# Before the layer norms of a two-layer trunk: three weight tiles kept, the second half's last products in two narrow banks, epsilon added early

## The chip, the core and the metric

The kernel runs on one core of a Trainium2 chip. The engines that matter are TensorE (PE in the profile; its weight loads are listed apart as PEld), VectorE (DVE), ScalarE (ACT), GpSimd (POOL) and SyncE (SP), whose queue issues nearly all transfers from memory. The metric is device time in microseconds, the median of several runs. Products add up in PSUM, which this kernel uses as eight banks of 512 columns (f32); everything else lies in SBUF.

## The reference, cut to what matters

One sequence of 256 tokens with 2048 features goes through two layers. Each layer has a token mixer (forgetting attention in layer 0, sliding-window attention in layer 1) and a gated feed-forward block with a short convolution. Behind each of these four sublayers stands a residual with a gate and a layer norm:

```python
x = layer_norm(DEEPNORM_ALPHA * x + (1.0 + g1) * y, ln_mix_g[i], ln_mix_b[i])
h = x * (1.0 + sc2) + sh2
y = conv_ffn(h, ...)
x = layer_norm(DEEPNORM_ALPHA * x + (1.0 + g2) * y, ln_ffn_g[i], ln_ffn_b[i])

def layer_norm(x, g, b):
    mu = jnp.mean(xf, axis=-1, keepdims=True)
    var = jnp.mean(jnp.square(xf - mu), axis=-1, keepdims=True)
    y = (xf - mu) * lax.rsqrt(var + LN_EPS)
    return y * g + b
```

`y` is the output of a matrix product (`w_o` of the mixer, `w_down` of the feed-forward block) with 2048 columns. The next sublayer's products need the normalised, modulated `h`, transposed. So at each of the four places all work of the next sublayer hangs on the last columns of the sublayer before. The fourth norm is followed by the output.

## The kernel before

**Tiles.** The tokens are two halves of 128 rows, `t = 0` and `t = 1` (`NT = 2`). Weights come in tiles of 256 x 512 (`wtile`, pool `wp` with ten slots, line 50). A tile holds two blocks of 128 rows and is called a pair here. Every f32 weight is split into a rounded high part and a remainder: ACT casts the tile to `wh` (line 285), VectorE subtracts to get `wl` (line 296), and both have four slots each in the pool `hl` (line 51). A product is then the sum of three: high by high, low by high, high by low (`x_mm`, lines 310 to 331). For one pair and one `t` that is six matmuls of 512 columns.

**The stream.** `stream` (line 277) issues a pair's transfer and its cast and puts its products into the list `work`; `settle` takes them from there with two pairs' lead, and emits the subtraction (`residual_`) some places ahead. Each `go` also makes one step of the list `post` (deferred work, such as the residual behind a product) and of `ada_tick`. The latter works on the modulation vectors in the background: one transfer `wa` and one VectorE accumulation into `acc` per step (lines 434 to 441). The next sublayer's transfers and casts are thus emitted before the last products of the present one. `spare` in `stream` puts `h` and `l` of the last `spare` pairs into the weight pool `wp` instead of `hl`.

**Order.** The tile framework schedules by priority, which is program order, with a model of the time, and sets all waits itself. `pin` keeps an instruction in program order among the pinned ones; others may be moved past them.

**The end of a product.** For the last of the four column blocks before a norm, `x_mm_end` (line 333) holds back the last `n` pairs: `t = 0` gets all its products first, then `t = 1` gets its products of the `n` pairs that were kept. `n` is 2 in `out_proj` (line 786) and in the first layer's feed-forward block, 6 in the second layer's (line 1162), where `spare` is 2.

**Residual and norm.** `residual` (line 654) does for each `t` of a column block of 512: a multiplication of the PSUM bank by the gate (line 660), an addition to `x` (661) and `bn_stats` (663), which gives count, mean and sum of squared deviations for the even and the odd elements. In the last block follow `bn_aggr` to mean and variance (666), the addition of epsilon (668), for `t = 0` the negated mean (670), the power -1/2 on POOL (671), and for `t = 0` on ACT the product of both (673). Only `t = 0` uses that product: it is normalised on ACT (`normalise`, line 687), `t = 1` on VectorE (line 689).

**The start of the next sublayer.** `modulate` (line 534) has a fixed, pinned order on PE: ten filler matmuls on ones (`warm`, tile name `warm`), the four transposes of `t = 0` (line 545), six fillers, the four transposes of `t = 1`, two fillers, then the first products. ACT (512) and VectorE (513, 516) turn the transposes into `hH` and `hL`. The rest of the features follow pair by pair between the products (`feed_`). Behind it, `affine` (line 700) loads rows of the norm's weights (`ln`, line 696) into four slots of `wp`.

**The output.** Behind the fourth norm, lines 1186 to 1195 do two VectorE operations per `t` and block of 512 (1190, 1194) and store the result; nothing there is pinned.

**PSUM.** `x_banks` takes two banks, one for each `t`, for a column block.

Of the kernel before, what the change touches and what calls it, by code (L numbers as in the profile page):

```python
# [10 lines left out]
F32 = mybir.dt.float32  # L11
# [3 lines left out]
ALU = mybir.AluOpType  # L15
AX = mybir.AxisListType

P = 128
D = 2048
# [13 lines left out]
EPS = 1e-5  # L33
# [8 lines left out]
def hybrid_trunk(ctx: ExitStack, tc: tile.TileContext, a: dict, out: bass.AP):  # L42
# [20 lines left out]
    def ttile(name="t"):  # L63
        return tp.tile([P, 2 * S], F32, tag="t", name=name)
# [7 lines left out]
    def x_banks():  # L72
        return [bank("xs") for _ in range(NT)]

    def mm(o, lhsT, rhs, start=False, stop=False, **kw):
        return nc.tensor.matmul(o, lhsT, rhs, start=start, stop=stop, **kw)  # L76
# [233 lines left out]
    def x_mm(ps, kc, h, l, stat, last, first=0, ts=range(NT)):  # L310

        if fresh[0]:
            fresh[0] = False
            for w in (h, l):
                for i in range(2):
                    for t in ts:
                        mm(ps[t], stat(kc + i, t)[0], w[:, i, :], start=w is h and kc + i == first)
            feed()
            for i in range(2):
                for t in ts:  # L320
                    mm(ps[t], stat(kc + i, t)[1], h[:, i, :], stop=kc + i == last)
            return
        for t in ts:
            for i in range(2):
                xh, xl = stat(kc + i, t)
                mm(ps[t], xh, h[:, i, :], start=kc + i == first)
                mm(ps[t], xl, h[:, i, :])
        feed()
        for t in ts:
            for i in range(2):  # L330
                mm(ps[t], stat(kc + i, t)[0], l[:, i, :], stop=kc + i == last)

    def x_mm_end(ps, stat, nk, n):

        kept = []

        def use(kc, h, l):
            end = kc >= nk - 2 * n
            x_mm(ps, kc, h, l, stat, nk - 1, ts=(0,) if end else range(NT))
            if end:  # L340
                kept.append((kc, h, l))
            if kc + 2 >= nk:
                for e in kept:
                    x_mm(ps, *e, stat, nk - 1, ts=(1,))

        return use

    def w_mm(ps, kc, h, l, last=KC - 1, first=0):
# [6 lines left out]
        for i, f, o in cells:  # L355
            mm(o, l[:, i, f * P:(f + 1) * P], hH[:, kc + i, :], stop=kc + i == last, skip_group_check=True)

    def x_stationary(wsrc, col, k0, nk, stat, end=0):

        ps = x_banks()  # L360
        use = x_mm_end(ps, stat, nk, end) if end else lambda kc, h, l: x_mm(ps, kc, h, l, stat, nk - 1)
        stream(wsrc, k0, col, list(range(nk)), use, max(end - 4, 0))
        return ps

    def w_stationary(wsrc, col):
# [279 lines left out]
                due = lambda cb=cb, acc=acc: chunk(cb, acc, bank("cps"))  # L645


    stats = cst.tile([P, NT, D // 512, nc.vector.BN_STATS_DIM], F32, name="stats")
    mhalf = cst.tile([P, 1], F32, name="mhalf")
    nc.gpsimd.memset(mhalf, -0.5)  # L650

# [2 lines left out]
    def residual(ps, d, gate, last):  # L654
        c0 = d * 512
        end = last and d == D // 512 - 1
        for t in range(NT):
            tmp = ttile()
            xs = x[:, t, c0:c0 + 512]
            pin(nc.vector.tensor_tensor(tmp, ps[t], gate[:, c0:c0 + 512], op=ALU.mult), end)  # L660
            pin(nc.vector.tensor_tensor(xs, xs, tmp, op=ALU.add), end)
            if last:
                pin(nc.vector.bn_stats(stats[:, t, d, :], xs), end)
            if end:
                mv = sp.tile([P, 2], F32, tag="mv", name="mv")
                pin(nc.vector.bn_aggr(mv, stats[:, t].rearrange("p a b -> p (a b)")))
                rs = sp.tile([P, 2], F32, tag="rs", name="rs")
                pin(nc.vector.tensor_scalar_add(rs[:, 0:1], mv[:, 1:2], EPS))
                if t == 0:
                    pin(nc.vector.tensor_scalar_mul(rs[:, 1:2], mv[:, 0:1], -1.0))  # L670
                nc.gpsimd.tensor_tensor(rs[:, 0:1], rs[:, 0:1], mhalf, op=ALU.pow)
                if t == 0:
                    nc.scalar.mul(rs[:, 1:2], rs[:, 1:2], rs[:, 0:1])
                moments[t] = (mv[:, 0:1], rs[:, 0:1], rs[:, 1:2])
            yield
# [101 lines left out]
    def out_proj(oT, full, w_o, l):  # L777
        def stat(kc, t):
            while kc not in full:
                step()  # L780
            return oT[kc][0][:, t * P:(t + 1) * P], oT[kc][1][:, t * P:(t + 1) * P]

        ps = {d: x_banks() for d in range(2)}

        def part(d, ks):
            use = x_mm_end(ps[d], stat, KC, 2) if d == D // WB - 1 else                 lambda kc, h, l_: x_mm(ps[d], kc, h, l_, stat, KC - 1)
            stream(w_o, 0, d * WB, ks, use)

        for i, ks in enumerate((range(0, 8), range(8, 12))):
            then(lambda i=i: ada.update(rate=((1.4,1.4,1.8,1.8), (0.9,)*4)[l][i]))  # L790
            for d in range(2):
                part(d, list(ks))
        then(lambda: ada_need(l, 2))
        for d in range(D // WB):
            if d < 2:
                part(d, list(range(12, KC)))
            else:
                then(lambda d=d: ada.update(rate=((1.4,1.4,1.8,1.8), (0.9,)*4)[l][d]))
                ps[d] = x_banks()
                part(d, list(range(KC)))  # L800
            then(lambda d=d: defer(residual(ps[d], d, gates[l, 2], True)))
        then(lambda: (flush(), ada.update(gate_free=True)))
# [293 lines left out]
    def conv_ffn(l):  # L1096
# [42 lines left out]
        for si, (b0, b1) in enumerate(sbs):  # L1139
            gT = []  # L1140
            then(lambda: ada.update(rate=(0.52, 0.4)[l]))
            for b in range(b0, b1):
                ps = w_stationary(w_up, b * WB)
                sil = [ttile("sil") for _ in range(2)]
                then(lambda ps=ps, b=b, sil=sil: defer(evac(ps, b * 4, silu(sil))))
                ps = w_stationary(w_up, DFF + b * WB)
                then(lambda ps=ps, b=b, sil=sil, gT=gT: defer(evac(ps, DFF // P + b * 4, gated(sil, gT))))

            def stat(kc, t, gT=gT):
                while kc >= len(gT):  # L1150
                    run_post()
                return gT[kc][:, 0, t * P:(t + 1) * P], gT[kc][:, 1, t * P:(t + 1) * P]

            def ready(si=si):
                if si == 0:
                    drain()
                ada_need(l, 5)
                ada["rate"] = (0.8, 0.4)[l]

            then(ready)  # L1160
            for d in range(D // WB):
                ps = x_stationary(w_dn, d * WB, b0 * 4, (b1 - b0) * 4, stat, (2, 6)[l] if si > 0 and d == D // WB - 1 else 0)
                then(lambda ps=ps, d=d, si=si: defer(residual(ps, d, gates[l, 5], si == len(sbs) - 1)))
        then(lambda: (flush(), ada.update(gate_free=True)))

# [56 lines left out]
```

## Time and profile before

| | us |
|---|---|
| median of 3 runs | 2248.07 (2247.27 to 2249.3) |
| the profiled execution | 2247.84 |
| its span, first to last instruction | 2246.1 |

The profile page shows one execution; its span is 1.74 us shorter than the time of that execution, which covers what lies around the instructions. Busy times overlap between engines. A group's line in the profile gives line, engine, operation, output and input, sizes, count, then busy time, mean duration in ns, the idle time of the engine just before, and what ended it. In the timeline the columns are start, duration, engine, line, operation, tiles, sizes, count, and in brackets the idle time before with its releaser; instructions of one kind are merged, and a merged entry's duration runs from the first start to the last end. The chain that ended last is followed back from the last instruction, each step to what released it, or to the instruction before it on its engine.

### The profile page before, as it was taken

The numbers are of one execution on the slowest core, as the hardware profiler recorded it, in microseconds if no ns is written. First come the engines' busy times: TensorE is split into PE (matmuls) and PEld (weight loads), VectorE is DVE, ScalarE is ACT, GpSimd is POOL, SyncE is SP. The second block draws the span as 40 slices with busy tenths as digits, with TensorE's granted clock in tenths as the row PEclk, the third lists the DMA queues.
The fourth block names the chain that finished last, engine by engine and source line by source line (L and its number), as shares of the span: only waits on it lengthen the run. The fifth ranks groups of instructions, "written<-read, shape, count | busy, mean of one in ns | idle before, by whom it ended". The sixth has DMA issues, their size and how long they took to land.

```text
span 2246.1 us, 33371 instructions
## 1 busy us (share of the span) xinstructions
PE 2199.2 (98%) x12206; PEld 1890.7 (84%) x12206; DVE 1854.0 (83%) x2689; ACT 1194.2 (53%) x1873; POOL 19.9 (1%) x51
## 2 busy tenths in 40 slices
PE   6999999999999999999999999999999999999997
PEld 6988998788888888888888788888888888888886
DVE  7989998889988968978988989889988655676766
ACT  4546654356655533555534578646655533555542
POOL 0000000000000000000000000000000000000000
PEclk9999999999999999999999999999999999999999
DMA  9998999868978889878887867678887556666553
GB/s 352 392 366 304 349 374 353 315 230 310 311 243 270 318 293 332 287 226 286 282 304 282 277 208 257 221 266 287 288 266 242 186 192 193 188 189 194 189 193 116
DMA packets 287429, 602.68 MB, mean 268 GB/s; under 512 B 21846, under 2 KB 55576, under 8 KB 286752
## 3 DMA queue, kind: packets, MB, share of 16 engines
q1 hardware_dynamic: 286208, 595.86, 77.9%
q0 software_dynamic: 1056, 4.69, 0.6%
q8 instruction: 95, 1.56, 0.3%
q14 instruction: 70, 0.57, 0.1%
HBM read 598.37 MB, written 2.10 MB: 267 GB/s over the span
## 4 chain that ended last, share of the span: by engine, by line
PE 81%; DVE 8%; DMA 7%; ACT 2%; issue 2%; SPq 0%; POOL 0%; DVEq 0%; ACTq 0%
PE wd L76 43%; PE xs L76 31%; DMA wo<-in_ada_w_dram 3%; DVE acc L440 3%; DVE wl L296 2%; PE ws L76 2%; DMA w<-in_fox_w_in_dram 2%; PE sm L76 1%; PE o L76 1%; PE S L76 1%; ACT wh L285 1%; PE warm L76 1%; DVE pr L736 0%; PE T L760 0%; ACT pr L748 0%
## 5 line engine op out<-in xcount | busy, mean ns | idle before, releaser
L285 ACT CAST wh<-w 128x1024 fp32r<-128x1024 f32 x728 | 765.3, 1052 | 789.5 <-PE wd L76 282.9
L296 DVE TENSOR_TENSOR wl<-w,wh 128x1024 fp32r<-128x1024 f32 x728 | 887.9, 1222 | 297.4 <-ACT wh L285 276.1
L76 PE MATMUL wd<-hHL,wh 128*128 128x512 f32 (+1 forms) x2832 | 718.2, 395 | 0.2
L76 PEld LDWEIGHTS wd<-hHL,wh 128*128 128x128 f32 x2832 | 504.6, 188 | 98.5 <-issue 2.9
L76 PEld LDWEIGHTS wd<-hHL,wl 128*128 128x128 f32 x2816 | 373.4, 188 | 31.0
L440 DVE SCALAR_TENSOR_TENSOR acc<-wa,cact,acc 128x1024 f32<-128x1024 f32 x300 | 380.6, 1278 | 0.0
L76 PE MATMUL wd<-hHL,wl 128*128 128x256 f32 x2816 | 380.0, 277 | 0.0
L76 PE MATMUL xs<-wh,gT 128*128 128x512 f32 x1408 | 350.0, 390 | 0.0
L76 PEld LDWEIGHTS xs<-wh,gT 128*128 128x128 f32 x1408 | 263.4, 188 | 54.2
L76 PE MATMUL xs<-wl,gT 128*128 128x512 f32 x704 | 189.6, 389 | 0.0
L76 PE MATMUL xs<-wh,hHL 128*128 128x512 f32 x704 | 186.7, 401 | 2.8 <-DVE hHL L86 2.6
L76 PEld LDWEIGHTS xs<-wl,gT 128*128 128x128 f32 x704 | 132.1, 188 | 27.6
L76 PEld LDWEIGHTS xs<-wh,hHL 128*128 128x128 f32 x704 | 128.9, 190 | 29.2 <-DVE hHL L86 3.4
L76 PE MATMUL ws<-hHL,wh 128*128 128x256 f32 x1024 | 133.7, 283 | 9.2 <-ACT wh L285 6.9
L1109 ACT ACTIVATE u<-s,ccol 128x256 f32<-128x256 f32 x176 | 104.8, 600 | 68.3 <-DVE s L1104 49.7
L76 PEld LDWEIGHTS ws<-hHL,wh 128*128 128x128 f32 x1024 | 125.4, 190 | 13.2 <-ACT wh L285 8.9
L76 PE MATMUL xs<-wh,oT 128*128 128x512 f32 x384 | 98.8, 395 | 0.1
L76 PE MATMUL xs<-wl,hHL 128*128 128x512 f32 x352 | 97.6, 397 | 0.6 <-DVE wl L296 0.6
L590 DVE SCALAR_TENSOR_TENSOR oacc<-wo,cact,oacc 128x512 f32<-128x512 f32 x111 | 79.7, 747 | 15.5 <-DMA wo<-in_ada_w_dram 11.0
L1110 DVE SCALAR_TENSOR_TENSOR u<-s,ccol,u 128x255 f32<-128x255 f32 x176 | 84.1, 480 | 5.7 <-ACT u L1109 5.7
L1112 DVE SCALAR_TENSOR_TENSOR u<-s,ccol,u 128x254 f32<-128x254 f32 x176 | 84.0, 478 | 1.1
L76 PEld LDWEIGHTS xs<-wh,oT 128*128 128x128 f32 x384 | 69.9, 188 | 13.9 <-ACT pT L762 0.6
(223 smaller groups left out, 1637.9 us busy)
## 6 DMA issues: line engine op xcount, KB each, us to landing
w<-in_ffn_w_up_dram SPq DMA_DIRECT2D x352, 512.0 KB, 4.6
wa<-in_ada_w_dram SPq DMA_DIRECT2D x320, 512.0 KB, 5.1
w<-in_ffn_w_down_dram SPq DMA_DIRECT2D x176, 512.0 KB, 4.4
w<-in_fox_w_in_dram SPq DMA_DIRECT2D x96, 512.0 KB, 6.6
wo<-in_ada_w_dram SPq DMA_DIRECT2D x128, 256.0 KB, 6.7
w<-in_swa_w_in_dram SPq DMA_DIRECT2D x40, 512.0 KB, 4.9
w<-in_fox_w_o_dram SPq DMA_DIRECT2D x32, 512.0 KB, 6.2
w<-in_swa_w_o_dram SPq DMA_DIRECT2D x32, 512.0 KB, 5.2
```

The source lines that it names most:

```text
L76: return nc.tensor.matmul(o, lhsT, rhs, start=start, stop=stop, **kw)
L285: pin(nc.scalar.copy(h, w), False)
L296: pin(nc.vector.tensor_tensor(l, w, f32(h), op=ALU.subtract), go in behind or tied[0] > 0)
L440: pin(nc.vector.scalar_tensor_tensor(ac, wo, cact[:, k:k + 1], ac, op0=ALU.mult, op1=ALU.add), True)
L590: nc.vector.scalar_tensor_tensor(ac, wk, cact[:, kc:kc + 1], ac, op0=ALU.mult, op1=ALU.add)
L1109: nc.scalar.activation(u, s, AF.Identity, bias=cw(CW, f), scale=cw(2, f))
L1110: nc.vector.scalar_tensor_tensor(u[:, 1:], s[:, :S - 1], cw(1, f), u[:, 1:], op0=ALU.mult, op1=ALU.add)
L1112: nc.vector.scalar_tensor_tensor(u[:, 2:], s[:, :S - 2], cw(0, f), u[:, 2:], op0=ALU.mult, op1=ALU.add)
```

## The change

Four things are changed.

- `x_mm_end` gives `t = 1` three banks. The products of all but the last `n` pairs go to `ps[1]`, which is closed there. Those of the last `n` pairs go to `ps[2]` (columns 0 to 255, all `n` pairs) and after that to `ps[3]` (columns 256 to 511, all `n` pairs). The number of weight loads and products doubles there, at half the columns.
- `n` is 3 instead of 2 in `out_proj` and in the first layer's feed-forward block; of the three, one pair's `h` and `l` lie in the weight pool (`SPARE`). The second layer's stays at 6, with two.
- `residual` of the last block has four pieces in place of two: `t = 1`'s earlier products (multiplied and added to `x`, no statistics), `t = 0`, `t = 1`'s first 256 columns, `t = 1`'s last 256 columns. `t = 1` has five groups of statistics instead of four, so `stats` grows.
- Epsilon is added, multiplied by the number of features, to the first sum of squared deviations right behind the first block's `bn_stats`, once per norm and `t`. The power then reads the variance directly. The negated mean of `t = 0` is made on ACT instead of VectorE.

```diff
--- before.py
+++ after.py
@@ -328,20 +328,28 @@
         feed()
         for t in ts:
             for i in range(2):
-                mm(ps[t], stat(kc + i, t)[0], l[:, i, :], stop=kc + i == last)
+                mm(ps[t], stat(kc + i, t)[0], l[:, i, :], stop=kc + i == (last[t] if isinstance(last, dict) else last))
 
     def x_mm_end(ps, stat, nk, n):
 
+        k0 = nk - 2 * n
+        H = WB // 2
         kept = []
 
+        def half(j, kc, h, l):
+            c = slice(j * H, (j + 1) * H)
+            x_mm({1: ps[2 + j][:, :H]}, kc, h[:, :, c], l[:, :, c], stat, nk - 1, first=k0, ts=(1,))
+
         def use(kc, h, l):
-            end = kc >= nk - 2 * n
-            x_mm(ps, kc, h, l, stat, nk - 1, ts=(0,) if end else range(NT))
-            if end:
-                kept.append((kc, h, l))
+            if kc < k0:
+                x_mm(ps, kc, h, l, stat, {0: nk - 1, 1: k0 - 1})
+                return
+            x_mm(ps, kc, h, l, stat, nk - 1, ts=(0,))
+            kept.append((kc, h, l))
             if kc + 2 >= nk:
-                for e in kept:
-                    x_mm(ps, *e, stat, nk - 1, ts=(1,))
+                for j in range(2):
+                    for e in kept:
+                        half(j, *e)
 
         return use
 
@@ -355,11 +363,13 @@
         for i, f, o in cells:
             mm(o, l[:, i, f * P:(f + 1) * P], hH[:, kc + i, :], stop=kc + i == last, skip_group_check=True)
 
+    SPARE = {0: 0, 3: 1, 6: 2}
+
     def x_stationary(wsrc, col, k0, nk, stat, end=0):
 
-        ps = x_banks()
+        ps = x_banks() + (x_banks() if end else [])
         use = x_mm_end(ps, stat, nk, end) if end else lambda kc, h, l: x_mm(ps, kc, h, l, stat, nk - 1)
-        stream(wsrc, k0, col, list(range(nk)), use, max(end - 4, 0))
+        stream(wsrc, k0, col, list(range(nk)), use, SPARE[end])
         return ps
 
     def w_stationary(wsrc, col):
@@ -645,7 +655,7 @@
                 due = lambda cb=cb, acc=acc: chunk(cb, acc, bank("cps"))
 
 
-    stats = cst.tile([P, NT, D // 512, nc.vector.BN_STATS_DIM], F32, name="stats")
+    stats = cst.tile([P, NT, D // 512 + 1, nc.vector.BN_STATS_DIM], F32, name="stats")
     mhalf = cst.tile([P, 1], F32, name="mhalf")
     nc.gpsimd.memset(mhalf, -0.5)
 
@@ -654,21 +664,27 @@
     def residual(ps, d, gate, last):
         c0 = d * 512
         end = last and d == D // 512 - 1
-        for t in range(NT):
-            tmp = ttile()
-            xs = x[:, t, c0:c0 + 512]
-            pin(nc.vector.tensor_tensor(tmp, ps[t], gate[:, c0:c0 + 512], op=ALU.mult), end)
+        if end:
+            pieces = [(1, ps[1], 0, 512, None), (0, ps[0], 0, 512, d), (1, ps[2], 0, 256, d), (1, ps[3], 256, 512, d + 1)]
+        else:
+            pieces = [(t, ps[t], 0, 512, d) for t in range(NT)]
+        for t, p, a0, a1, st in pieces:
+            n = a1 - a0
+            tmp = ttile()[:, :n]
+            xs = x[:, t, c0 + a0:c0 + a1]
+            pin(nc.vector.tensor_tensor(tmp, p[:, :n], gate[:, c0 + a0:c0 + a1], op=ALU.mult), end)
             pin(nc.vector.tensor_tensor(xs, xs, tmp, op=ALU.add), end)
-            if last:
-                pin(nc.vector.bn_stats(stats[:, t, d, :], xs), end)
-            if end:
+            if last and st is not None:
+                pin(nc.vector.bn_stats(stats[:, t, st, :], xs), end)
+                if d == 0:
+                    nc.vector.tensor_scalar_add(stats[:, t, 0, 2:3], stats[:, t, 0, 2:3], D * EPS)
+            if end and st is not None and (t == 0 or a1 == 512):
                 mv = sp.tile([P, 2], F32, tag="mv", name="mv")
-                pin(nc.vector.bn_aggr(mv, stats[:, t].rearrange("p a b -> p (a b)")))
+                pin(nc.vector.bn_aggr(mv, stats[:, t, :st + 1].rearrange("p a b -> p (a b)")))
                 rs = sp.tile([P, 2], F32, tag="rs", name="rs")
-                pin(nc.vector.tensor_scalar_add(rs[:, 0:1], mv[:, 1:2], EPS))
                 if t == 0:
-                    pin(nc.vector.tensor_scalar_mul(rs[:, 1:2], mv[:, 0:1], -1.0))
-                nc.gpsimd.tensor_tensor(rs[:, 0:1], rs[:, 0:1], mhalf, op=ALU.pow)
+                    nc.scalar.mul(rs[:, 1:2], mv[:, 0:1], -1.0)
+                nc.gpsimd.tensor_tensor(rs[:, 0:1], mv[:, 1:2], mhalf, op=ALU.pow)
                 if t == 0:
                     nc.scalar.mul(rs[:, 1:2], rs[:, 1:2], rs[:, 0:1])
                 moments[t] = (mv[:, 0:1], rs[:, 0:1], rs[:, 1:2])
@@ -783,8 +799,11 @@
         ps = {d: x_banks() for d in range(2)}
 
         def part(d, ks):
-            use = x_mm_end(ps[d], stat, KC, 2) if d == D // WB - 1 else                 lambda kc, h, l_: x_mm(ps[d], kc, h, l_, stat, KC - 1)
-            stream(w_o, 0, d * WB, ks, use)
+            end = 3 if d == D // WB - 1 else 0
+            if end:
+                ps[d] += x_banks()
+            use = x_mm_end(ps[d], stat, KC, end) if end else lambda kc, h, l_: x_mm(ps[d], kc, h, l_, stat, KC - 1)
+            stream(w_o, 0, d * WB, ks, use, SPARE[end])
 
         for i, ks in enumerate((range(0, 8), range(8, 12))):
             then(lambda i=i: ada.update(rate=((1.4,1.4,1.8,1.8), (0.9,)*4)[l][i]))
@@ -1159,7 +1178,7 @@
 
             then(ready)
             for d in range(D // WB):
-                ps = x_stationary(w_dn, d * WB, b0 * 4, (b1 - b0) * 4, stat, (2, 6)[l] if si > 0 and d == D // WB - 1 else 0)
+                ps = x_stationary(w_dn, d * WB, b0 * 4, (b1 - b0) * 4, stat, (3, 6)[l] if si > 0 and d == D // WB - 1 else 0)
                 then(lambda ps=ps, d=d, si=si: defer(residual(ps, d, gates[l, 5], si == len(sbs) - 1)))
         then(lambda: (flush(), ada.update(gate_free=True)))
 
```

## The prediction

> **What bounds the kernel now.** I read the page first, then the chain that ended last around each layer norm, then the same microseconds instruction by instruction.
>
> ```profile
> span 2246.1 us, 33371 instructions
> PE 2199.2 (98%) x12206; PEld 1890.7 (84%) x12206; DVE 1854.0 (83%) x2689; ACT 1194.2 (53%) x1873; POOL 19.9 (1%) x51
> ```
>
> PE is busy 98% of the span. A change that adds and removes no products can win only where PE waits, or where it runs work of no use. The change is placed at four such spots: three norms inside (around 465, 1217 and 1494 us) and the last one before the output. The chain around the first:
>
> ```profile
> 461.81 3.67 PE xs L76 x16
> 465.48 2.27 PE warm L76 x10
> 467.75 0.44 PE sm L545 x4
> 468.19 1.40 PE warm L76 x6
> 469.58 0.23 PE sm L545 x2
> 469.84 1.04 DVE t L513 x2
> ```
>
> Columns are start, duration, engine and line. The chain goes from the last products (16 in 3.67 us, 0.229 each) straight through ten filler matmuls, four transposes of the first half of the rows (t = 0) and six fillers, to the transposes of t = 1. It does not go through VectorE's residual and moments. They run beside it:
>
> ```profile
> 462.76 0.69 DVE L660 TENSOR_TENSOR t<-xs,gate 128x512 f32<-128x512 f32 x1 [1.34 <-PE xs L76]
> ...
> 465.31 2.44 PE L76 MATMUL warm<-ones 128*128 128x512 f32 x10
> ...
> 465.51 0.69 DVE L660 TENSOR_TENSOR t<-xs,gate 128x512 f32<-128x512 f32 x1
> ...
> 467.70 0.26 DVE L666 BATCH_NORM_AGGREGATE mv<-stats 128x2 f32<-128x24 f32 x1
> ...
> 467.99 0.15 DVE L668 TENSOR_SCALAR rs<-mv 128x1 f32<-128x1 f32 x1
> 468.24 0.57 POOL L671 TENSOR_TENSOR rs<-rs,mhalf 128x1 f32<-128x1 f32 x1 [1.02 <-DVE rs L668]
> 468.84 0.74 DVE L689 TENSOR_SCALAR x<-x,mv,rs 128x256 f32<-128x256 f32 x2 [0.70 <-POOL rs L671]
> 469.31 0.52 PEld L545 LDWEIGHTS sm<-ident,x 128*128 128x128 f32 x4 [0.16 <-DVE x L689]
> ```
>
> The last line decides: after the fillers PE waits for VectorE's normalised t = 1 for 0.16 us only. At the second and third norm it is hardly more:
>
> ```profile
> 1221.27 0.52 PEld L545 LDWEIGHTS sm<-ident,x 128*128 128x128 f32 x4 [0.17 <-DVE x L689]
> ```
>
> ```profile
> 1498.66 0.53 PEld L545 LDWEIGHTS sm<-ident,x 128*128 128x128 f32 x4 [0.22 <-DVE x L689]
> ```
>
> The diff leaves the fillers as they are, so these 0.16 + 0.17 + 0.22 = 0.55 us are all that an earlier t = 1 can give there.
>
> **The products.** Three pairs of weight tiles are kept instead of two (six before the output, as before). Of t = 1, 18 products of 512 columns become 36 of 256, in two banks; before the output 36 become 72. The price of a narrow product and of an operation on 256 columns:
>
> ```profile
> 231.37 2.73 PE ws L76 x24
> ```
>
> ```profile
> L1104 DVE TENSOR_TENSOR s<-wd,s 128x256 f32<-128x256 f32 x176 | 71.0, 418 | 0.0
> ```
>
> 24 products of 256 columns, each with a weight load of its own, took 2.73 us, 0.114 each: half of 0.229. So PE's time does not change; I cost the split at nothing. The cover is that each of the added weight loads runs under the product before it; without it see the rivals.
>
> **VectorE at norms one and three.** Call 465.31, where PE begins the fillers, E. Before, t = 1's three operations start at 465.51 and the aggregate at 467.70: 2.19 us, 0.73 each. With 256 columns (418 ns, and the 0.03 us that stands between the aggregate and the next line) they take 0.45 each. The aggregate then starts 0.20 + 1.35 = 1.55 us after E, the power, with the addition of epsilon gone, at 1.55 + 0.26 + 0.10 = 1.91, the normalisation 0.60 later, as before: E + 2.5 where it was E + 3.5. **One microsecond is saved on VectorE, but PE arrives at these transposes at 469.15, E + 3.84, whatever VectorE does.** VectorE then stands idle.
>
> The t = 0 work comes 1.36 us earlier (three pairs, 18 x 0.227 = 4.1 us of products behind it rather than 2.7). Its normalised chunk is wanted at 467.75, with more than a microsecond to spare. The new first piece (t = 1's earlier products, a multiplication and an addition, 2 x 0.73 = 1.46 us) falls into VectorE's idle time: 1.34 us before 462.76 in the row above, and at the third norm
>
> ```profile
> 1489.47 1.23 DVE L296 TENSOR_TENSOR wl<-w,wh 128x1024 fp32r<-128x1024 f32 x1 [1.35 <-ACT wh L285]
> 1492.05 0.69 DVE L660 TENSOR_TENSOR t<-xs,gate 128x512 f32<-128x512 f32 x1 [1.35 <-PE xs L76]
> ```
>
> The negated mean, now on ACT, runs beside POOL's power. Norms one and three: -0.16 and -0.22 us.
>
> **VectorE at norm two** is full before t = 0 ends:
>
> ```profile
> 1206.77 1.23 DVE L296 TENSOR_TENSOR wl<-w,wh 128x1024 fp32r<-128x1024 f32 x1 [0.45 <-ACT wh L285]
> 1207.91 2.48 DVE L440 SCALAR_TENSOR_TENSOR acc<-wa,cact,acc 128x1024 f32<-128x1024 f32 x2
> 1210.30 1.22 DVE L296 TENSOR_TENSOR wl<-w,wh 128x1024 fp32r<-128x1024 f32 x1
> 1212.21 1.23 DVE L296 TENSOR_TENSOR wl<-w,wh 128x1024 fp32r<-128x1024 f32 x1 [0.69 <-ACT wh L285]
> 1213.35 1.28 DVE L440 SCALAR_TENSOR_TENSOR acc<-wa,cact,acc 128x1024 f32<-128x1024 f32 x1
> 1214.75 0.69 DVE L660 TENSOR_TENSOR t<-xs,gate 128x512 f32<-128x512 f32 x1
> ```
>
> The accumulations of L440 and the residual's pieces are pinned, so they keep their order; the pieces come behind 1213.35. At best that accumulation ends 0.45 + 0.69 us earlier, at 1213.5 (the third kept pair's copies lie in the weight pool, so the next weights get their slots, and casts, a pair earlier). Then: first piece 1.46, t = 0 2.19 + 0.29, first half 1.35, second half 1.35: 1220.1. Aggregate and power 0.36 + 0.60, normalisation and load 0.47: the transposes of t = 1 start at 1221.6 instead of 1221.27, **+0.3 us**. If none of the idle time is won back it is +1.4; with the accumulation behind the pieces it is the floor, -0.17. I take +0.3.
>
> **The end.** Here no filler stands in the way, but VectorE has work all the time:
>
> ```profile
> 2226.62 0.69 DVE L660 TENSOR_TENSOR t<-xs,gate 128x512 f32<-128x512 f32 x1 [6.75 <-PE xs L76]
> ...
> 2229.23 1.41 DVE L1190 SCALAR_TENSOR_TENSOR x<-x,mv,ln 128x512 f32<-128x512 f32 x2
> ...
> 2234.78 0.69 DVE L660 TENSOR_TENSOR t<-xs,gate 128x512 f32<-128x512 f32 x1 [0.17 <-PE xs L76]
> ...
> 2237.33 1.41 DVE L1190 SCALAR_TENSOR_TENSOR x<-x,mv,ln 128x512 f32<-128x512 f32 x2
> ...
> 2241.30 1.54 DVE L1194 SCALAR_TENSOR_TENSOR x<-x,rs,ln 128x512 f32<-128x512 f32 x3
> ```
>
> From 2226.62 to 2242.84 it is idle once, 0.17 us before 2234.78. The first piece disappears in the 6.75 us before. The first half, ready some 4.1 us before the products end, comes between t = 0's output operations and pushes them behind. So the sum of the work counts: 6 x 0.45 - 3 x 0.73 = +0.51; two epsilon additions and a negation gone, -0.21 (0.07 each from start to start); the idle 0.17 filled: **+0.1 us**.
>
> The eight early additions of epsilon, 0.15 each by the row at 467.99, lie in the first column block's residual, under PE's products.
>
> **The slots.** The third pair's two copies hold two of the weight pool's ten slots until E. SyncE's queue shows what that delays:
>
> ```profile
> 458.73 0.37 SPq L283 DMA_DIRECT2D w<-in_ffn_w_up_dram  x1
> 461.45 0.34 SPq L696 DMA_DIRECT2D ln<-in_ln_mix_g_dram  x1
> 475.03 0.34 SPq L696 DMA_DIRECT2D ln<-in_ln_mix_b_dram  x1
> ```
>
> The transfer issued at 461.45 is followed by none until 475.03, since no slot is released meanwhile. Two transfers move from before E to just after it, and land before 475. Behind them on SyncE are loads that wait anyway. Price nothing; bound below.
>
> **Sum:** -0.16 + 0.3 - 0.22 + 0.1 = 0.0 us. The profiled execution took 2247.84 us, 1.74 more than its span and 0.23 less than the median of 2248.07; so the forecast is **2248.1 us, no change**. Less than 0.2% (4.5 us) cannot be told from no change here.
>
> **Rivals.**
> - *VectorE's saving comes through everywhere*: 3 x 1.0 us and, at the end, 2.55 (2234.78 to 2237.33) to 1.66 (0.20 less, 3 x 0.45 and 0.29), 0.9: -3.9, 2244.2 us. For it: VectorE's residual is the last wait before each transpose. Against: that wait is 0.16 to 0.22 us. 8%.
> - *More than that*, with the next stage's waits gone as well because casts come earlier. PE is idle 4.1 us in the stage behind the second norm, by this row:
>
> ```profile
> 1222.00:1441.00 219.00, 214.88 (x1105) 175.62 (x1104) 195.13 (x440) 163.41 (x393) 1.21 (x4) 1.00 0.69 233
> ```
>
>   With all of it 2240 us. 3%.
> - *VectorE's fixed order (slower)*: at norm two none of the idle time is won back, +1.4 instead of +0.3; and the first half is put ahead of t = 0's first output operation. That half is ready at 2230.7, VectorE free at 2229.1: 1.6 us idle. Together 2250.8 us. It decides once the first piece at norm two starts after 1213.5. For it: the pinned order. Against: at 2229.23 unpinned output work did pass the pinned residual. 17%.
> - *The held slots (slower)*: a product needs a weight whose transfer waited for E. From the median time to landing,
>
> ```profile
> w<-in_ffn_w_up_dram SPq DMA_DIRECT2D x352, 512.0 KB, 4.6
> ```
>
>   up to 4.6 us at each of one to three norms: 2253 to 2262. Against: the weights read behind E are in before 461. 5%.
> - *Weight loads bound the halves (slower)*:
>
> ```profile
> L76 PEld LDWEIGHTS ws<-hHL,wh 128*128 128x128 f32 x1024 | 125.4, 190 | 13.2 <-ACT wh L285 8.9
> ```
>
>   Were the loads not overlapped, 36 x 0.19 = 6.8 instead of 4.1 us at each norm, twice that at the end: +13.5, 2262. Against: 0.114 us per load and product in the row at 231.37. 2%. The Trainium skill, "TensorE: Matmul & The Clock Gate", section "Back-to-back issue gap", speaks for such a loss: in a stream of loads and products it gives about 81 ns for 128 columns and 131 for 512, so by a straight line (an estimate) 98 for 256, and two halves would cost 65 ns more than the whole. This trace has 229 and 114 and does not show it.
>
> **How the numbers follow.** The forecast has 65%; its own range is 2246.5 to 2249.5 (norm two from -0.17 to +0.8, and the 2 us between the runs shown). The range of 2244.0 to 2251.5 takes in the first and the third rival and leaves out 10%, which I round up for what I cannot price: the scheduler draws the whole order behind the first norm anew. Faster by over 0.2%: the second rival, 3%. Slower: the last two, 7%. Within: 90%.
>
> **What would show it.** Right: t = 1's normalisation starts about E + 2.5 at the first and third norm, and the transposes' load has no wait left, with the ten and six fillers between as before; at the end L1190 of t = 1 starts not before 2237. Wrong: fewer or other PE work between E and the transposes; VectorE idle between 2229 and 2231; a wait of a cast for a DMA just behind a norm; products of 256 columns spaced by more than 0.12 us.

## The result and the profile after

| | before | after |
|---|---|---|
| median, us | 2248.69 (2247.27 to 2249.45, 4 runs) | 2272.19 (2271.47 to 2275.17, 4 runs) |
| profiled execution, us | 2247.84 | 2272.16 |
| its span, us | 2246.1 | 2270.4 |

The ratio is 1.0109, 95% interval 1.0097 to 1.0121: the changed kernel is 24 us slower, where no change was forecast. The head of the page of the changed kernel:

```profile
span 2270.4 us, 33572 instructions
...
PE 2222.8 (98%) x12296; PEld 1916.3 (84%) x12296; DVE 1861.9 (82%) x2705; ACT 1193.4 (53%) x1877; POOL 20.1 (1%) x51
```

PE has 90 products more, since 90 old ones were halved, and is still busy 98% of a longer span. The granted clock is 0.996 in both. So PE did not get gaps; it is slower, or it starts late. The chain that ended last shows where. It passes the ten fillers of each inner norm, in both kernels. Before (the first such row, at 465.48, stands in the prediction; columns are start, duration, engine, line):

```profile
1217.44 2.27 PE warm L76 x10
...
1494.77 2.27 PE warm L76 x10
```

After:

```profile
476.68 2.29 PE warm L76 x10
...
1235.01 2.31 PE warm L76 x10
...
1512.97 2.29 PE warm L76 x10
```

The changed kernel is 11.2 us late when it arrives at the *first* of the changed places, 17.6 at the second, 18.2 at the third and 24.3 at the end (2270.4 less 2246.1). Between the second and the third place, where the second mixer runs, only 0.6 us are lost. The rest goes in three long stages: 11.2 us ahead of the first norm, 6.4 in the first feed-forward block, 6.1 in the second. Up to its last column block such a stage holds nothing of the edit but small additions of epsilon. The norms themselves are not where the time went.

**The two feed-forward stages.** Groups of instructions by shape, before:

```profile
L76 PE MATMUL wd<-hHL,wh 128*128 128x512 f32 x2800 | 713.5, 396 | 0.2
L76 PE MATMUL wd<-hHL,wl 128*128 128x256 f32 x2816 | 380.0, 277 | 0.0
```

and after:

```profile
L76 PE MATMUL wd<-hHL,wh 128*128 128x512 f32 x2800 | 713.4, 396 | 0.2
L76 PE MATMUL wd<-hHL,wl 128*128 128x256 f32 x2816 | 392.6, 281 | 0.0
```

`wd` is the bank of the feed-forward blocks' up products. Here the split weights `wh` and `wl` are loaded into the array, and the activations `hHL` are streamed past them: 512 columns (high and low) past `wh`, 256 (high alone) past `wl`. The same 2816 products of 256 columns with `wl` took 12.6 us longer, and the 2800 of 512 columns with `wh` did not. 6.4 + 6.1 = 12.5: this group is both feed-forward stages' loss. By stage, all products into `wd` together take 6.2 us more in the first block (494.7 to 500.9) and 6.2 in the second (493.0 to 499.2). The count, the shape and the neighbours are as before.

**Ahead of the first norm.** The first 160 us of both kernels (stretch, length, busy time of PE, PEld, DVE, ACT and POOL with counts, granted clock, busy share of the DMA engines, GB/s), before:

```profile
0.00:160.00 160.00, 138.33 (x977) 127.61 (x978) 132.33 (x184) 72.44 (x92) 6.40 (x25) 0.99 1.03 368
```

and after:

```profile
0.00:160.00 160.00, 136.81 (x917) 125.33 (x918) 124.99 (x173) 69.73 (x89) 3.86 (x20) 0.98 1.03 345
```

This stage is bound by transfers: their engines are fully busy in both, and moved 345 instead of 368 GB/s. No instruction of the edit has run by then: VectorE's order is that of the kernel before until 412 us, PE's until 458 us, and that of SyncE's transfers for the whole run. Most of the 11.2 us are lost in this stretch: the product that starts at 163 us in the kernel before starts 9.3 us later in the changed one.

What differs from the first microsecond on is where things lie. `stats` grew from 192 to 240 bytes per partition; it is placed in steps of 32 bytes, so 64 more are taken, and every tile that was allocated behind it moved up by 64. The addresses of the built programs, as start modulo 256:

```
                                      before  after
hHL   activations, high and low         192    192
acc, gate                               160    224
wp    weight tiles as they land           0     64
hl    split weights wh, wl                0     64
gp    later activations (gT, oT, qT)      0     64
tp    temporaries                         0     64
```

Theory A: the edit's instructions are worth nothing, as forecast, and the 24 us are the price of these addresses. The rivals, called theory B in the first four expectations, are the edit itself, and the order that the scheduler draws anew behind 412 us.

### The profile page after: what moved, and what is told of

It reads as the page before. It is cut to its first block, busy times and chain, and to the rows that moved or that the text cites. A ratio compares the mean times of both kernels' runs of the same rounds, so it can differ in the third digit from the quotient of the medians.

```text
span 2270.4 us, 33572 instructions
## 1 busy us (share of the span) xinstructions
PE 2222.8 (98%) x12296; PEld 1916.3 (84%) x12296; DVE 1861.9 (82%) x2705; ACT 1193.4 (53%) x1877; POOL 20.1 (1%) x51
## 4 chain that ended last, share of the span: by engine, by line
PE 83%; DMA 7%; DVE 6%; ACT 2%; issue 1%; SPq 0%; DVEq 0%; ACTq 0%
PE wd L76 43%; PE xs L76 31%; DMA wo<-in_ada_w_dram 5%; PE ws L76 4%; DVE wl L296 2%; PE sm L76 1%; DVE acc L450 1%; DMA w<-in_fox_w_in_dram 1%; PE S L76 1%; PE o L76 1%; PE warm L76 1%; PE T L776 0%; ACT wh L285 0%; DVE pr L752 0%; DMA wa<-in_ada_w_dram 0%
## 5 line engine op out<-in xcount | busy, mean ns | idle before, releaser
L76 PE MATMUL wd<-hHL,wh 128*128 128x512 f32 (+1 forms) x2832 | 718.2, 395 | 0.2
L76 PEld LDWEIGHTS wd<-hHL,wh 128*128 128x128 f32 x2832 | 506.5, 188 | 98.0 <-issue 2.9
L76 PEld LDWEIGHTS wd<-hHL,wl 128*128 128x128 f32 x2816 | 382.8, 188 | 31.5
L76 PE MATMUL wd<-hHL,wl 128*128 128x256 f32 x2816 | 392.6, 281 | 0.0
L76 PE MATMUL xs<-wh,gT 128*128 128x512 f32 (+1 forms) x1444 | 352.2, 384 | 0.0
L76 PEld LDWEIGHTS xs<-wh,gT 128*128 128x128 f32 x1444 | 266.7, 188 | 52.9
L76 PE MATMUL xs<-wh,hHL 128*128 128x512 f32 (+1 forms) x720 | 188.8, 398 | 2.8 <-DVE hHL L86 2.6
L76 PE MATMUL xs<-wl,gT 128*128 128x512 f32 (+1 forms) x722 | 191.5, 384 | 0.0
L76 PEld LDWEIGHTS xs<-wl,gT 128*128 128x128 f32 x722 | 134.4, 188 | 27.0
L76 PEld LDWEIGHTS xs<-wh,hHL 128*128 128x128 f32 x720 | 130.4, 190 | 29.7 <-DVE hHL L86 3.4
L76 PE MATMUL ws<-hHL,wh 128*128 128x256 f32 x1024 | 139.1, 288 | 10.8 <-ACT wh L285 7.4
L76 PEld LDWEIGHTS ws<-hHL,wh 128*128 128x128 f32 x1024 | 129.9, 193 | 15.9 <-ACT wh L285 10.5
L76 PE MATMUL xs<-wh,oT 128*128 128x512 f32 (+1 forms) x392 | 99.5, 391 | 0.2 <-ACT pT L778 0.2
L76 PE MATMUL xs<-wl,hHL 128*128 128x512 f32 (+1 forms) x360 | 98.2, 391 | 0.4 <-DVE wl L296 0.4
L76 PEld LDWEIGHTS xs<-wh,oT 128*128 128x128 f32 x392 | 70.7, 188 | 13.9 <-ACT pT L778 0.6
```

## The experiments

Each group of runs has runs of the kernel before on the same chip beside it: median 2247.77 us for e1 to e4, 2248.24 for e5 to e8, 2247.93 for e9 and e10, 2247.98 for e11 and e12; the ratios are taken against these. Spans are compared with the 2246.1 of before. Behind `hHL` the code has a tile called `gap` (line 494, 96 bytes) that nothing reads or writes; it only takes room, and its size is a handle on all addresses behind it.

### e1: the whole change, at the old addresses

```diff
-    cst.tile([P, 24], F32, name="gap")
+    cst.tile([P, 8], F32, name="gap")
```

(on the changed kernel: 64 bytes less in front, `wp` and all behind it where they were)

> The changed kernel whole; only the unused tile named gap, which lies just ahead of stats, is cut from 96 to 32 bytes per partition. The larger stats takes 256 bytes instead of 192, so every pool behind it is back at the addresses of before: the weight pool starts at byte 77312, a multiple of 256, instead of 77376. Theory A (the 64 bytes cost the 24 us): back to 2248 us, within 2 us of before; what remains of a difference is the change that was meant. Theory B (the new order, the held slots, the narrow products cost it): stays at 2272 us, 24 us above before.

2249.22 us (2246.82 to 2251.44), ratio 1.0004 (0.9995 to 1.0013), span 2246.0. The chain:

```profile
465.27 2.27 PE warm L76 x10
...
1217.48 2.29 PE warm L76 x10
...
1494.78 2.29 PE warm L76 x10
```

All three within 0.21 us of before, though every edited instruction is there. The edit costs nothing and gains nothing that these runs can tell; the interval leaves room for 0.13%, about 3 us.

### e2: the kernel before, 64 bytes up

```diff
-    cst.tile([P, 24], F32, name="gap")
+    cst.tile([P, 40], F32, name="gap")
```

(on the kernel before; no instruction differs but in its addresses, here and in e3 to e8, e11 and e12)

> The kernel before, no instruction changed; only the unused tile gap grows by 64 bytes, so that the weight pool and all pools behind it lie at the addresses of the changed kernel. Theory A: 2272 us, +24 us, with the first norm some 11 us later and some 6 us more in each feed-forward block. Theory B: 2248 us, no difference.

2272.11 us, ratio 1.0108 (1.0094 to 1.0122), span 2270.1. Of its groups by shape:

```profile
L76 PE MATMUL wd<-hHL,wl 128*128 128x256 f32 x2816 | 392.7, 282 | 0.0
```

The whole loss, without the change, down to the same group. With e1 this settles the question of the cause. The rest of the runs ask what it is about the addresses.

### e3 and e4: the loss in two parts

e3 leaves the weight pool where it was and moves what lies behind it; e4 moves the weight pool (and the small tiles, `acc` and `gate` in front of it) and puts what lies behind it on a multiple of 256 again.

```diff
 # e3: between the weight pool and the pool of the split weights
+    pad = ctx.enter_context(tc.tile_pool(name="pad", bufs=1))
+    pad.tile([P, 16], F32, name="pad")
 # e4: the same with [P, 48], and gap of [P, 40]
```

> The kernel before; the weight pool (the target of the weight transfers) stays where it was, and 64 unused bytes between it and the pool of the split weights shift that pool and all behind it. Theory A in two parts: the transfers are as before, so the first norm is at its old time (465 us, at most 1 us off); TensorE's weight loads read tiles 64 bytes off, so about +6 us in each feed-forward block: about 2261 us. If the transfers alone cost the time: 2248 us. Theory B: 2248 us.

> The kernel before; the weight pool is 64 bytes off, and 192 more unused bytes behind it put the pool of the split weights and all behind it back on a multiple of 256. Theory A in two parts: the transfers write 64 bytes off, so the first norm comes some 11 us later, and the feed-forward blocks, whose weight loads read aligned tiles, are as before: about 2259 us. If the weight loads alone cost the time: 2248 us. Theory B: 2248 us.

e3: 2262.94 us, ratio 1.0069 (1.0054 to 1.0085), span 2260.9, +14.8. Its chain and its group (the two added lines make L76 to L78):

```profile
467.42 2.29 PE warm L78 x10
```

```profile
L78 PE MATMUL wd<-hHL,wl 128*128 128x256 f32 x2816 | 392.6, 282 | 0.0
```

e4: 2257.44 us, ratio 1.0043 (1.0029 to 1.0056), span 2256.2, +10.1. Its chain, its group and its first 160 us:

```profile
475.64 2.27 PE warm L78 x10
```

```profile
L78 PE MATMUL wd<-hHL,wl 128*128 128x256 f32 x2816 | 380.2, 277 | 0.0
```

```profile
0.00:160.00 160.00, 132.12 (x912) 121.01 (x913) 124.80 (x173) 69.47 (x89) 3.86 (x20) 0.98 1.03 345
```

The two parts are separate and add up: 14.8 + 10.1 = 24.9, against 24.0 in e2. e4 has the slow opening (345 GB/s, first norm 10.2 us late) and nothing else; e3 arrives only 1.9 us late and has the slow products, 12.6 us of its 14.8. The engines that read the weight tiles are not what slows e4's opening: until 460 us a subtraction on VectorE takes 1217 ns in e4 and 1219 in before, a cast on ACT 1046 and 1051.

### e5 and e6: 32 and 128 bytes

The `gap` of e2 with `[P, 32]` and `[P, 56]`: is a step of 32 free, or one of 128?

> The kernel before with 32 unused bytes more ahead of stats: the weight pool and all behind it 32 bytes off a multiple of 256. Theory A1 (what counts is whether a tile starts on a multiple of 256 bytes): as slow as with 64 bytes, 2272 us (first norm about 11 us later, 6 us more in each feed-forward block). Theory A2 (the cost grows with the distance, or 64 is special): a clearly other time between 2248 and 2272 us.

> The kernel before with 128 unused bytes more ahead of stats: the weight pool and all behind it on an odd multiple of 128. Theory A1 (multiples of 256 count, for transfers and for weight loads): 2272 us. Theory A3 (multiples of 128 suffice for both): 2248 us. If they suffice for one of the two only: about 2258 us (transfers slow, first norm 11 us later, feed-forward blocks as before) or 2262 us (weight loads slow, first norm within 2 us of its old time).

e5: 2273.74 us, ratio 1.0111 (1.0096 to 1.0127), span 2271.6. e6: 2253.92 us, ratio 1.0024 (1.0014 to 1.0034), span 2252.3, a time that no theory had named. The opening is late in both by about as much as in e2. The chain of e5, then that of e6:

```profile
476.58 2.32 PE warm L76 x10
```

```profile
476.22 2.30 PE warm L76 x10
```

So for the opening any of the three offsets from a multiple of 256 is as bad as any other. What saves e6 comes later: its groups by shape are another mixture,

```profile
L76 PE MATMUL wd<-hHL,wh 128*128 128x512 f32 x2800 | 703.4, 393 | 0.1
...
L76 PE MATMUL wd<-hHL,wl 128*128 128x256 f32 x2816 | 385.0, 278 | 0.0
```

those with `wl` 5.0 us slower than before, those with `wh` 10.1 us *faster*.

### e7 and e8: two wrong guesses

e7 moves only what lies behind the split weights (a pad of `[P, 16]` between `hl` and `gp`). The guess was that `wh` and `wl` cost by their own address, so that nothing would happen. e8 puts `hHL` itself on a multiple of 256, with all behind it at the old addresses:

```diff
+    cst.tile([P, 16], F32, name="gap0")
     hHL = cst.tile([P, KC, 2, S], F32R, name="hHL")
...
-    cst.tile([P, 24], F32, name="gap")
+    cst.tile([P, 8], F32, name="gap")
```

> The kernel before; weight pool and the pool of the split weights stay, 64 unused bytes between that pool and the next shift only the pools of the activations, of the temporaries and of the small tiles. If the time of the third experiment came from TensorE's weight loads of split weights: 2248 us, no difference, and the products of 256 columns with wl at 277 ns. If it came from any of the other pools (ACT's and VectorE's operands, the gated activations as stationary operands): about 2262 us.

> The kernel before; hHL, the modulated activations, starts at byte 25280, 192 past a multiple of 256, in the kernel before and in the changed one; here 64 unused bytes ahead of it put it on a multiple of 256, and the gap behind it is cut by as much, so nothing else moves. hHL is the moving operand of 512 and 256 columns in the feed-forward up products, and the stationary operand only of products of 512 columns. If the start address matters to weight loads alone and shows only under narrow products: no difference, 2248 us. If it matters to moving operands too: faster, by up to some 6 us in each feed-forward block, about 2236 us.

e7: 2263.45 us, ratio 1.0064 (1.0047 to 1.008), span 2262.5, +16.4. The guess falls, but not because those products were slow again. In e7:

```profile
L78 PE MATMUL wd<-hHL,wl 128*128 128x256 f32 x2816 | 380.1, 277 | 0.0
L78 PE MATMUL xs<-wh,gT 128*128 128x512 f32 x1408 | 358.9, 396 | 0.0
L78 PE MATMUL xs<-wl,gT 128*128 128x512 f32 x704 | 194.1, 396 | 0.0
```

and before:

```profile
L76 PE MATMUL xs<-wh,gT 128*128 128x512 f32 x1408 | 350.0, 390 | 0.0
L76 PE MATMUL xs<-wl,gT 128*128 128x512 f32 x704 | 189.6, 389 | 0.0
```

`wd` is fast, and the feed-forward blocks' down products, which took 350.0 to 350.2 us with `wh` in e2 to e6, are 8.9 + 4.5 = 13.4 us slower. In e2 and in the changed kernel `gT` lies 64 up as well, and these products are not slow there, since `wh` and `wl` lie 64 up too.

e8: 2255.82 us, ratio 1.0031 (1.0019 to 1.0043), span 2254.7. Its span is 8.6 us longer with `hHL` *better* aligned. Its groups:

```profile
L76 PE MATMUL wd<-hHL,wh 128*128 128x512 f32 x2800 | 706.1, 394 | 0.1
L76 PE MATMUL wd<-hHL,wl 128*128 128x256 f32 x2816 | 394.1, 283 | 0.0
```

Neither tile has a good address of its own. Sorted by the *distance* between the two, start of the loaded tile less start of the streamed tile, modulo 256, the rows fall into place:

```
 wh/wl loaded, hHL streamed     distance   with wl    with wh
 before, e1, e4, e7                 64    380.0-380.2  713.5-713.8
 e5                                 96    390.4        716.4
 after, e2, e3                     128    392.6-392.7  713.4-713.6
 e6                                192    385.0        703.4
 e8                                  0    394.1        706.1
 gT loaded, wh streamed
 before, e2 to e6, e8                0    350.0-350.2
 e7                                 64    358.9
```

Equal distances agree within 0.4 us. For `gT` and `wh` the rows at distance 0 have four different addresses (both tiles at 0, 32, 64 or 128); for `hHL` and the weights, equal distances are so far equal addresses modulo 256, which e11 changes. The theory of the distance: the time of these products goes by that distance, and the opening by the offset of the tiles that the transfers fill.

### e11 and e12: the theory of the distance, tried on two new layouts

e11 is e8's `gap0` alone: `hHL` and everything behind it 64 up, all distances as before. e12 is e3's pad with `[P, 32]`: weight pool as before, distance 192.

> The kernel before with 64 bytes put ahead of hHL, so that hHL and everything behind it lies 64 bytes higher: the pools lie where they lie in the slow kernels, but every distance between hHL, the split weights and the activations is that of the kernel before. Read from the runs so far: the time of a product goes by the distance between the address of what it multiplies and the address of what it is loaded with (wd with wl: 380.0 us for 64 bytes, 392.6 for 128, 394.1 for 0). Theory of the distance: wd with wl 380 us, xs from gT 350 us, only the opening transfers late, first filler of norm 1 at about 476, time about 2258. Rival, each tile's own address counts: wd with wl 390 or more as in the other kernels with the split weights 64 bytes up, time about 2270.

> The kernel before with 128 bytes put between the weight pool and the pool of the split weights: weight tiles where they were, split weights and activations 128 bytes higher, so hHL and the split weights have the distance that they had with 128 bytes ahead of everything. Theory of the distance with separate opening: opening on time (fillers of norm 1 at 465 to 468), wd with wh 703 us (713.5 before), wd with wl 385 us (380.0 before), projections from hHL some 3 us more, sum -10 + 5 + 3: span about 2244, time about 2246 or somewhat under (2243 if the projections do not count), below both kernels. Rival, a step of 128 costs by itself as with 128 bytes ahead of everything: about 2254.

e11: 2257.11 us, ratio 1.0042 (1.0028 to 1.0055), span 2254.4; 2258 was expected of the distance, 2270 of each tile's own address. Groups, and the first 160 us:

```profile
L76 PE MATMUL wd<-hHL,wl 128*128 128x256 f32 x2816 | 380.0, 277 | 0.0
L76 PE MATMUL xs<-wh,gT 128*128 128x512 f32 x1408 | 350.0, 390 | 0.0
```

```profile
0.00:160.00 160.00, 133.30 (x929) 123.05 (x930) 126.00 (x174) 70.32 (x90) 3.86 (x20) 0.98 1.04 347
```

`wl` lies where it lay in e2, and the group takes 380.0 us, not 392.7. Only the slow opening is left; the first fillers come at 473.81, 2 us earlier than expected.

e12: 2245.42 us (2243.9 to 2246.73), ratio 0.9988 (0.9979 to 0.9996), span 2243.0. About 2246 or somewhat under was expected. Its chain and its groups:

```profile
467.17 2.30 PE warm L78 x10
```

```profile
L78 PE MATMUL wd<-hHL,wh 128*128 128x512 f32 x2800 | 703.2, 393 | 0.1
...
L78 PE MATMUL wd<-hHL,wl 128*128 128x256 f32 x2816 | 384.9, 278 | 0.0
```

The opening is 1.7 us late, the groups change by -10.3 and +4.9, and 1.7 - 10.3 + 4.9 = -3.7 is near the -3.1 of the spans. The 3 us that were expected for the projections are not in this sum: the second mixer's stage, between the fillers of the second and the third norm (1216.42 and 1494.28), is only 0.5 us longer. It is the fastest layout tried, by 0.12% with an interval that just excludes no difference, and it is the kernel before with 128 unused bytes put in.

### e9 and e10: do the fillers hide what the change saves?

The prediction said that VectorE's microsecond is lost because PE comes through its fillers at E + 3.84 in any case. e9 is e1 with four fillers fewer per norm, e10 the kernel before with the same:

```diff
-        warm(10)
+        warm(9)
...
-            warm(6 - 4 * t)
+            warm(3 - t)
```

> The changed kernel at the old addresses, with nine fillers instead of ten ahead of the transposes of t = 0 and three instead of six ahead of those of t = 1, at each of the three inner norms: 4 x 0.227 = 0.9 us of PE's fixed work less. Theory F (at the inner norms PE's fillers, not VectorE, end last in the changed kernel): the transposes of t = 1 begin about 0.8 us earlier after the last product, -2.5 us in all, about 2246 us. Rival (something else ends last, a VectorE or ACT step behind the transposes): no difference from the changed kernel at the old addresses, 2248 to 2249 us, and PE idle longer.

> The kernel before with the same fillers taken away. Theory F: before the change VectorE ends 0.2 us behind PE, so taking fillers away moves only idle time, and nothing is won: within 0.3 us at each norm, about 2248 us, and the wait for the normalised t = 1 grows from 0.2 to about 1 us at each of the three norms. Rival (fillers cost time whatever VectorE does): -2.7 us, about 2245 us.

2248.08 us, ratio 0.9999 (0.999 to 1.0008), and 2247.9 us, ratio 0.9999 (0.999 to 1.0008): the times do not tell them apart, and the 2246 us expected of e9 did not come. The timelines of the first norm do (start, duration, engine, line, operation, tiles, idle time before). e9:

```profile
466.06 2.20 PE L76 MATMUL warm<-ones 128*128 128x512 f32 x9
...
469.09 0.53 PEld L555 LDWEIGHTS sm<-ident,x 128*128 128x128 f32 x4
...
470.61 0.74 PE L76 MATMUL wd<-hHL,wh 128*128 128x256 f32 x4 [0.29 <-ACT hHL L522]
```

e10:

```profile
467.03 2.21 PE L76 MATMUL warm<-ones 128*128 128x512 f32 x9
...
471.02 0.76 PE L545 MATMUL sm<-ident,x 128*128 128x128 f32 x4 [0.65 <-DVE x L689]
```

In e10 PE only exchanges fillers for a wait of 0.65 us for VectorE's normalised rows; these transposes start 3.99 us behind the first filler, as their load did before (4.00). In e9 the load comes 3.03 us behind the first filler, 0.84 earlier than in e1 (3.87). But the first product of the next stage, which then waits for ACT, comes 4.55 us behind the first filler. In e1 that was 5.02, by its own timeline below and this row:

```profile
470.13 0.74 PE L76 MATMUL wd<-hHL,wh 128*128 128x256 f32 x4
```

So the fillers do hide the saving, but what appears without four of them is 0.47 us at this norm and not 1.0, too little for these measurements.

## Why the prediction was wrong

**The step that failed** is the line "Sum: -0.16 + 0.3 - 0.22 + 0.1 = 0.0 us". Its four terms are all instructions and waits at the norms. It has no term for memory layout, although the description of the change names the cause ("so `stats` grows"), and so it takes for granted that every untouched product and transfer keeps its time. The missing term is +24: about 10 through slower transfers in the opening (e4) and about 13 through slower products (12.6 of e3's 14.8), each of them far from any edited line. The 10% left out of the range was justified with the scheduler's order behind the first norm; that order was not the trouble either: the kernel was 11 us late by the time the orders part, and e1, which has the new order, is not late.

**The mechanics at the norms held**, as e1 shows, where nothing else disturbs them. Its timeline at the first norm:

```profile
465.11 2.43 PE L76 MATMUL warm<-ones 128*128 128x512 f32 x10
...
467.68 0.74 DVE L705 TENSOR_SCALAR x<-x,mv,rs 128x256 f32<-128x256 f32 x2 [0.70 <-POOL rs L687]
...
468.98 0.59 PEld L555 LDWEIGHTS sm<-ident,x 128*128 128x128 f32 x4
...
469.63 1.03 DVE L523 TENSOR_SCALAR t<-sm,G,B 128x256 f32<-128x256 f32 x2 [1.22 <-PE sm L555]
```

- *The saving on VectorE*: `t = 1`'s normalisation at E + 2.57 (E + 2.5 forecast, + 3.5 before). The load of the transposes has no wait left, all fillers are there, and VectorE then idles 1.22 us for PE. The microsecond is won on VectorE and lost to the fillers, as forecast.
- *Norm two*: +0.3 was forecast, because the pieces would start at 1213.5 at best. They start at 1213.05, since the accumulation ahead of them ended earlier still, and the load comes no later than before (1221.27):

```profile
1213.05 0.68 DVE L675 TENSOR_TENSOR t<-xs,gate 128x512 f32<-128x512 f32 x1
...
1221.20 0.59 PEld L555 LDWEIGHTS sm<-ident,x 128*128 128x128 f32 x4
```

- *The split products*: 36 of them from 460.95 to the filler at 465.11 are 4.16 us, 0.116 each, against 0.114 forecast. The first of them:

```profile
460.95 0.64 PE L76 MATMUL xs<-wh,oT 128*128 128x256 f32 x4
```

  The rival in which the added weight loads show (6.8 us) did not occur.
- *The end*: the first half's pieces come between `t = 0`'s output operations, and L1209 (L1190 of before) of `t = 1` starts at 2237.18, not before 2237. The last group starts 0.14 us earlier than before (2241.30) instead of 0.1 later:

```profile
2231.05 0.42 DVE L675 TENSOR_TENSOR t<-xs,gate 128x256 f32<-128x256 f32 x1
...
2237.18 1.42 DVE L1209 SCALAR_TENSOR_TENSOR x<-x,mv,ln 128x512 f32<-128x512 f32 x2
...
2241.16 1.54 DVE L1213 SCALAR_TENSOR_TENSOR x<-x,rs,ln 128x512 f32<-128x512 f32 x3
```

- *The held slots*, priced at nothing, cost nothing that e1's chain shows: 1217.48 and 1494.78 against 1217.44 and 1494.77.

The forecast of no change is therefore right for the edit and wrong for the kernel.

## What to carry to other kernels

A change that alters the size of any tile allocated ahead of the pools is two changes: the edit, and a new address for everything behind it. Measure them apart by giving the room back (e1) or by moving the unchanged kernel (e2), before reading anything into the edit. Where the chain that ended last is already late ahead of the first edited line, and a group of untouched products has another mean, look at addresses first.

## What the hardware showed that was not expected

- *A product's time goes by the distance of its two operands in SBUF.* In five distances the feed-forward blocks' 2816 products of 256 columns took 380.0 to 394.1 us, and the 2800 of 512 columns 703.2 to 716.4, not in the same order. The mixers' smaller groups do not follow the distance as closely: 384 products with `wh` and `oT` took 98.8 us in before and 100.0 in e4, at the same distance. The Trainium skill, "TensorE: Matmul & The Clock Gate", section "Step-by-step: what each phase is for", says that the streamed operand and the weight load have read ports of their own, so that loading the next weights takes no read bandwidth from the running product. These runs disagree in so far as the two are not independent: e8, e11 and before differ in no instruction, and the group is slow only where the distance is another. Why (shared banks, or something else) was not tried; three of the eight distances in steps of 32 were not either.
- *In the opening, transfers are slower when the tiles that they fill lie off a multiple of 256, and by how much they lie off does not matter.* 345 and 347 GB/s in e4 and e11 against 368 in the first 160 us; the first norm is 8.3 us late at the least (e11, 64 bytes, the row below) and 11.4 at the most (e2, 64 bytes), with 32 bytes (e5, 11.1) and 128 (e6, 10.7) between them:

```profile
473.81 2.31 PE warm L76 x10
```

  In the kernels with all ten fillers whose weight pool lies on a multiple of 256, these fillers come between 465.27 (e1) and 467.94 us (e8), so a difference of 2 us between openings means little, and one of 8 does. Behind the opening the loss is gone, though the same tiles are filled: a packet of 2048 bytes took 84 ns (median) in before and 88 with 32, 64 and 128 bytes (e5, e4, e6) in the first 160 us, but 84 in all four between 200 and 460 us, when no packets of 1024 bytes run beside them. Why it is only there was not tried.

  The Trainium skill, "DMA: Bandwidth & Descriptors", section "How a descriptor splits into AXI transactions", has a rule of this kind: a descriptor that does not start on a multiple of 256 bytes needs more beats. It tells it of what is read, while here the end that is written moved. An estimate from it for rows of 2048 bytes is 66 beats instead of 64 at an offset of 64 and 68 at 128, 3% and 6%, and twice that for rows of 1024 bytes, of which the opening has more. The trace agrees in direction, not in growth: it shows 6% at 64 (345 of 368) and no more at 128 (346 in e6), and none behind the opening. Not separated was how much of it belongs to the weight pool and how much to `acc` and `gate`, which move along with it.
- *A better alignment can be a loss* (e8, ratio 1.0031), and 128 bytes of nothing a small gain (e12, 0.9988).
